# Output projection of the last row tile placed ahead of the turning of four other tiles (hybrid decoder layer, one core)

## The chip, the cores and the metric

The kernel runs on one core of one Trainium2 chip. The metric is the device time in microseconds from the first to the last instruction of one execution. TensorE is called PE below, VectorE DVE, ScalarE ACT, GpSimd POOL and SyncE SP. Each engine works off its own instructions in a fixed order, and an instruction that waits holds up all that stand behind it on that engine. SP computes nothing here: it issues most of the loads, so its order is the order of a queue of loads.

## The reference

One layer of a decoder trunk: 1024 prompt rows (tiles 0 to 7 of 128 rows) and 64 sample rows (tile 8), 1024 features, fp32.

```python
def layer(h, p_l, ...):
    xn = rmsnorm(h, norm_mix)
    mix = token_mixers(xn, ...)        # two groups of heads, then: concat([o_ret, o_rw], -1) @ w_out
    h = h + mix
    h = h + peer(rmsnorm(h, norm_ffn), peer_wq, peer_keys, peer_u, peer_v)
    gate = sigmoid(rmsnorm(h, ple_norm) @ ple_gate)
    return h + gate * (p_l @ ple_proj)

def peer(xn, wq, keys, u_tab, v_tab):                  # 8 heads, 2 x 128 keys, 16 picks
    q = (xn @ wq).reshape(rows, 8, 2, 128)
    s = einsum('phcd,hcnd->phcn', q, keys)
    sv, si = top_k(s, 16)                              # then the best 16 of the 256 pairs: e, gsm
    hval = einsum('pd,phkd->phk', xn, u_tab[e])
    return einsum('phk,phkd->pd', gelu(hval) * gsm, v_tab[e])
```

The retention heads (`o_ret`) and the RWKV-7 heads (`o_rw`) of a tile need the state that the tile before leaves, so the tiles go through the mixers one after the other.

## The kernel before

**Stages.** First the mixers, tile by tile, tile 7 last. Beside them the rows of finished tiles go through `c_rows`: the output projection (`ewo`, 1024 x 1024 weights `cw`, loaded anew for each tile), the residual add, the store of the row to the DRAM array `hd`, the norm, and the store of the normed row to `xd`. Then the query stage: `c_query` runs over 16 half heads; for each it loads 512 KB of `wq` (`wqr`), splits it into a high part on ACT (`wqh`) and a low part on POOL (`wql`), multiplies it with the turned rows of six tiles (`pq`: 256 columns for group G1, tiles 2 and 3, and 512 columns for group G2, tiles 4 to 7) and scores it against the keys (`psc`); DVE then picks the best 16 (`MAX8`, `FIND_INDEX8`, `MATCH_REPLACE8`, lines 1043 to 1047). After it come the hidden stage and the dense stage, in which G2 is computed against all 16384 experts (`ph`, `py`), and the last stage, `ple`, tile by tile in the order 0, 1, 8, 4, 5, 6, 7, 2, 3.

**Turning.** The query needs the normed rows with features on the partitions, each split in two parts. `split_T` does it for one tile: eight 128 x 128 transposes on PE (`ntr`, line 326) into two PSUM banks of tag "a", and for each bank the high part on ACT (line 303) and the low part on DVE (line 305), both named `cx`. `rows_in` loads a tile's normed row from `xd` into a buffer `cxn` (line 1010) and turns it. Tag "a" has two PSUM banks, tag "b" three.

**The gather.** Tiles 0, 1, 8 and then 2, 3 go through the experts that they picked, one expert row at a time: POOL issues an indirect load of 512 KB (`grow`, line 1144) into one of about five buffers, DVE works it in with one instruction (line 1158 in the first pass, `gacc`, line 1172, in the second). One such piece of work is called a gather step here. The steps have the lowest priority of all, and a scheduler that works at build time on the order of emission and priorities puts them between the other instructions. That order is fixed when the kernel runs. A gather's result is stored (`yd`) and added to its tile's rows at line 1413 in `ple`.

**The seam.** The change is in what lies between tile 7's mixers and the query. The last vector operation of the mixers is line 989: `tail`, the gated RWKV half of tile 7's rows. The gate's matmul goes to a bank `pgt` of tag "a" (`PGT = "a"`), which is held until `tail` has read it. `tail` stays on the chip. Around it `build()` emits:

1. `rows_in` for G1 (tiles 2 and 3), with two `cxn` buffers (`CN = 2`);
2. `rest()`, the `c_rows` of the other late tiles, of which tile 6 is the last;
3. `c_rows` of tile 7, here called the last tile's rows. It differs from the others: all eight weight slabs `cw` (512 KB each, line 589) are loaded at once into buffers that the query uses later; the tile's residual row is loaded to `ch` (line 594, one of the two buffers of tag `uraw` that the query's `wqr` also uses); the row `od` of the retention half is loaded to `cot`; both halves are transposed (`etr`, line 604); the projection is 16 matmuls of 128 x 512 (line 611); DVE adds the two halves of the result to `ch` (line 613); `ch` is stored to `hd`, squared on ACT (`csq`, line 627), the norm's factor is made on POOL (`crs`, lines 297 and 298), DVE multiplies (line 633) and `split_T` turns `ch` itself (`ntr<-ch`);
4. between its steps, one tile of `rows_in` for tiles 4, 5 and 6;
5. the query, and then what is left of the early gathers.

`tail`, the eight `cw` and tile 7's `ch` meet in one more place: seven of the eight `cw` slabs go to buffers whose former content `tail`'s stage has to be done with, so that their loads wait for `tail`.

Of the kernel before, what the change touches and what calls it, by code (L numbers as in the profile page):

```python
# [8 lines left out]
F32 = mybir.dt.float32  # L9
# [8 lines left out]
D = 1024  # L18
# [164 lines left out]
G1 = [2, 3]  # L183
DW = 4
LW = 3
CN = 2
BORDER = [1, 8, 2, 3, 4, 5, 6, 7]
A0 = [0, 1]
A1 = [2, 3]
# [2 lines left out]
PGT = "a"  # L192
# [3 lines left out]
G2 = [4, 5, 6, 7]  # L196
# [9 lines left out]
def spans(tiles):  # L206

    e = [sum(SIZE[t] for t in tiles[:i]) for i in range(len(tiles) + 1)]
    return dict(zip(tiles, e)), e[-1]
# [8 lines left out]
class K:  # L218
# [360 lines left out]
    def c_rows(self, wp, t, ring=4, da=None, x=None):  # L579

        nc, I = self.nc, self.I
        n = SIZE[t]
# [18 lines left out]
        for k in range(2):  # L601
            p = self.ps("etr", "a").rearrange("p (a b) -> p a b", a=4)
# [4 lines left out]
        if da is not None:  # L607
            p = [self.ps("ewo", "b") for _ in range(2)]
            for k in range(8):
                for c in range(2):  # L610
                    nc.tensor.matmul(p[c][:n], oT[k // 4][:, k % 4, :n], ws[k][:, cs[c]], start=k == 0, stop=k == 7)
            for c in range(2):
                nc.vector.tensor_tensor(h[:n, cs[c]], p[c][:n], h[:n, cs[c]], op=OP.add)
        else:
            for c in range(2):
                p = self.ps("ewo", "a")
                for k in range(8):
                    w = half("cw")
                    nc.sync.dma_start(w, I['w_out'][k, :, cs[c]])
                    nc.tensor.matmul(p[:n], oT[k // 4][:, k % 4, :n], w, start=k == 0, stop=k == 7)  # L620
                    if k % 4 == 3:
                        yield
                nc.vector.tensor_tensor(h[:n, cs[c]], p[:n], h[:n, cs[c]], op=OP.add)
# [7 lines left out]
        for c in range(2):  # L631
            nc.sync.dma_start(gr[c], I['rows'][o + 512 * c:o + 512 * c + 512].partition_broadcast(128))
            nc.vector.scalar_tensor_tensor(h[:n, cs[c]], h[:n, cs[c]], r[:n], gr[c][:n], op0=OP.mult, op1=OP.mult)
        if x is not None:
            self.split_T(h, n, x[0], x[1], 0)
        else:
            nc.scalar.dma_start(self.xd[t][:n], h[:n])
# [66 lines left out]
    def rw_mix(self, t):  # L704
        nc, I, O, wp = self.nc, self.I, self.O, self.cw
        smp = t == 8
        n, o = SIZE[t], t * 128
# [3 lines left out]
        hb = "bd" if smp or first else "bb"  # L711
# [9 lines left out]
        p = self.ps("pz")  # L721
# [12 lines left out]
        for k in range(2):  # L734
            p = self.ps("pcs")[:, :258].rearrange("p (a b) -> p a b", a=2)
# [10 lines left out]
        p = self.ps("pa").rearrange("p (a b) -> p a b", a=4)  # L746
# [21 lines left out]
        p = self.ps("pbon")  # L768
# [70 lines left out]
        for li, m in enumerate(LEVELS):  # L839
# [4 lines left out]
            for s in range(2):  # L844
                p = self.ps("trz", hb[s]).rearrange("p (a b) -> p a b", a=4)
# [4 lines left out]
                p = self.ps("pG", hb[s])[:, :256].rearrange("p (h q) -> p h q", h=4)  # L850
# [5 lines left out]
            for s in range(2):  # L856
                p = self.ps("pZG", hb[s])[:, :256].rearrange("p (h q) -> p h q", h=4)
# [20 lines left out]
        p = self.ps("pX", "d")  # L878
# [12 lines left out]
        if smp:  # L891
            p = self.ps("pU", "d")
# [5 lines left out]
        else:  # L898
            lo, up = slice(0, 64), slice(64, 128)
            for half in (lo, up):  # L900
                if half is up:
                    p = self.ps("pL", "d")
# [5 lines left out]
                p = self.ps("pU", "d")  # L908
# [5 lines left out]
        if not smp:  # L914
            p = self.ps("pS", "d").rearrange("p (a b) -> p a b", a=4)
# [15 lines left out]
            if t == 7:  # L931
                p = self.ps("pso", "d").rearrange("p (a b) -> p a b", a=4)
# [7 lines left out]
        else:  # L940
# [6 lines left out]
            for h in range(8):  # L947
                hs = slice(h * 64, h * 64 + 64)
                p = self.ps("pss", "b")
# [32 lines left out]
        bv = T3("bv").rearrange("p (h d) -> p h d", h=8)  # L982
        nc.vector.tensor_tensor(bv[:n], V[:n].rearrange("p (h d) -> p h d", h=8), bon[:n, 8:16, None].to_broadcast([n, 8, 64]), op=OP.mult)
        eng.tensor_tensor(xc[:n], xc[:n], bv[:n], op=OP.add)
        p = self.ps("pgt", PGT or hb[0])
        nc.tensor.matmul(p[:n], sf13[:, :n], self.g2, start=True, stop=True)
        if t == 7:
            self.tail = self.ep0.tile([128, 512], F32, name="tail", tag="Wq", bufs=QB)
# [14 lines left out]

    def rows_in(self, wp, tiles, x):

        off, _ = spans(tiles)
        for t in tiles:
            n = SIZE[t]
            xn = wp.tile([128, D], F32, name="cxn", bufs=CN)
            self.nc.sync.dma_start(xn[:n], self.xd[t][:n])  # L1010
            self.split_T(xn, n, x[0], x[1], off[t])
            yield

    def c_query(self, wp, da, parts):
# [429 lines left out]
    def build(self):  # L1444
        PS = bass.MemoryType.PSUM
        run = lambda g: [None for _ in g]
        sb = lambda name, es, **kw: self.pool(name, es=es, reuse_waits="tile", **kw)
        with self.es:
            self.setup()
            em, ee, eg, et, ew, ex, ep, e0, e1, e2 = (ExitStack() for _ in range(10))  # L1450
# [26 lines left out]
            for _ in a:  # L1477
                for _ in range(IE):
                    next(early, None)
            e2.close()  # L1480
            late = self.group_b(BORDER, early)
            em.close()
            cq = sb("cq", ew, bufs=2, side="right")
            parts = [G1, G2]
            self.layout(cq, [(f"ss{g[0]}", [128, len(g), 128], F32, SB) for g in parts] +
                        [(f"qT{g[0]}", [128, spans(g)[1]], F32, 1) for g in parts])
            cn = sb("cn", ew, side="right")
            c1 = sb("cx1", ew, side="right")
            x1 = self.rows_of(c1, G1)
            cx = sb("cx2", ex)  # L1490
            x = self.rows_of(cx, G2)
# [8 lines left out]
            def rest():  # L1500
                for t in late[:-1]:
                    yield from self.c_rows(co, t, CRING)

            run(self.rows_in(cn, G1, x1))
            run(rest())
            last = self.c_rows(co, late[-1], CRING, da, [y[:, :, n3:] for y in x])
            next(last)
            for _ in self.rows_in(cn, G2[:-1], x):
                next(last, None)
            run(last)  # L1510
            run(query)
            run(early)
# [12 lines left out]
            with ExitStack() as e:  # L1525
# [9 lines left out]
                for i, t in enumerate(G2 + [None]):  # L1535
                    tk = self.topk(tp, t) if t is not None else iter(())
                    while True:
                        a, b = next(tk, "end"), next(gate, "end")
# [41 lines left out]
```

## Time and profile before

| | us |
|---|---|
| three runs: lowest, median, highest | 3747.6, 3758.44, 3776.36 |
| the profiled execution, its own time | 3747.65 |
| its span in the trace | 3745.9 |
| PE busy | 3294.1 (88%) |
| DVE busy | 2856.0 (76%) |
| POOL busy | 2336.2 (62%) |
| ACT busy | 1217.6 (33%) |

The span is 1.75 us shorter than the execution's own time, and the execution is one of the fastest of the runs. "Idle before" in a row of a trace is the time in which the engine stood still ahead of an instruction, and the arrow names what ended it. Rows of a timeline give the start and the duration, and several equal instructions in one row have a joint duration.

### The profile page before, as it was taken

How to read it: one execution, taken by the hardware profiler on the slowest of the kernel's cores; microseconds unless marked ns; L12 is line 12 of the kernel's file. 1: busy time of each engine (PE TensorE's matmuls, PEld its weight loads, DVE VectorE, ACT ScalarE, POOL GpSimd, SP SyncE). 2: the span in 40 equal slices, each digit the busy share in tenths (PEclk: the TensorE clock that was granted, in tenths of full speed). 3: DMA queues.
4: the chain of work that ended last, by engine and by line, in shares of the span. 5: the costliest groups of instructions: out<-in, count | busy, mean ns of one | idle time of the engine just before them, and what ended most of it. 6: DMA issues, size and time to landing. Idle time of an engine off the chain costs nothing. (4 is left out here: it accounts for less than half of the span.)

```text
span 3745.9 us, 52394 instructions
## 1 busy us (share of the span) xinstructions
PE 3294.1 (88%) x17749; PEld 2742.5 (73%) x17749; DVE 2856.0 (76%) x5655; ACT 1217.6 (33%) x2260; POOL 2336.2 (62%) x2068
## 2 busy tenths in 40 slices
PE   7799995868869978884899999998999999989979
PEld 7698994644747866673787888887888877767757
DVE  4454388878797698886897998875777787888885
ACT  4232220111202111211222788793333333333322
POOL 5364176455364555554558877867888888888751
PEclk9799995667968566876999999999999999999989
DMA  7266578889778877888769888899999999999982
GB/s 254 81 216 212 187 244 289 276 286 311 258 249 313 311 268 253 285 273 320 254 216 317 298 311 320 332 340 334 337 347 342 328 354 371 374 370 368 339 279 89
DMA packets 425286, 1077.84 MB, mean 288 GB/s; under 512 B 46459, under 2 KB 144505, under 8 KB 420346
## 3 DMA queue, kind: packets, MB, share of 16 engines
q0 software_dynamic: 165888, 604.05, 45.5%
q1 hardware_dynamic: 203102, 378.60, 30.6%
q10 hardware_dynamic: 56028, 91.84, 6.6%
q8 instruction: 141, 2.31, 0.2%
q14 instruction: 127, 1.04, 0.1%
HBM read 982.51 MB, written 91.75 MB: 287 GB/s over the span
## 5 line engine op out<-in xcount | busy, mean ns | idle before, releaser
L1144 POOL DMA_INDIRECT grow<-in_pv,eid x576 | 567.4, 985 | 464.1 <-DVE gacc L1172 289.0
L1144 POOL DMA_INDIRECT grow<-in_pu,eid x576 | 558.1, 969 | 405.6 <-DVE grow L1158 228.0
L1172 DVE SCALAR_TENSOR_TENSOR gacc<-grow,ac,gacc 128x1024 f32<-128x1024 f32 x571 | 731.8, 1282 | 87.0 <-DMA grow<-in_pv,eid 80.3
L1158 DVE SCALAR_TENSOR_TENSOR grow<-grow,gacc 128x1024 f32<-128x1024 f32 x576 | 691.6, 1213 | 131.0 <-DMA grow<-in_pu,eid 124.1
L332 PE MATMUL ph<-cx,uh 128*128 128x512 f32 x1024 | 406.3, 397 | 17.5 <-DVE al L305 9.8
L1318 PE MATMUL py<-ah,vh 128*128 128x512 f32 x1024 | 403.3, 394 | 19.7 <-ACT vh L303 19.7
L333 PE MATMUL ph<-cx,uh 128*128 128x512 f32 x1024 | 404.9, 395 | 0.0
L1319 PE MATMUL py<-al,vh 128*128 128x512 f32 x1024 | 402.4, 393 | 2.6 <-DVE al L305 2.6
L307 POOL TENSOR_TENSOR vl<-vraw,vh 128x640 fp32r<-128x640 f32 (+1 forms) x224 | 326.2, 1460 | 34.9 <-ACT vh L303 17.5
L307 POOL TENSOR_TENSOR ul<-uraw,uh 128x1024 fp32r<-128x1024 f32 x128 | 307.7, 2404 | 64.5 <-issue 26.8
L1321 PE MATMUL py<-ah,vl 128*128 128x512 f32 x1024 | 275.9, 397 | 11.4 <-POOL vl L307 11.1
L335 PE MATMUL ph<-cx,ul 128*128 128x512 f32 x1024 | 263.2, 395 | 2.9 <-POOL ul L307 2.9
L303 ACT ACTIVATE vh<-vraw 128x640 fp32r<-128x640 f32 (+1 forms) x224 | 154.9, 692 | 301.8 <-DMA vraw<-in_pvd 105.6
L1318 PEld LDWEIGHTS py<-ah,vh 128*128 128x128 f32 x1024 | 193.5, 189 | 68.5 <-ACT vh L303 27.0
L332 PEld LDWEIGHTS ph<-cx,uh 128*128 128x128 f32 x1024 | 194.5, 190 | 58.0 <-DVE al L305 10.2
L1321 PEld LDWEIGHTS py<-ah,vl 128*128 128x128 f32 x1024 | 191.5, 189 | 61.7 <-POOL vl L307 20.7
L1319 PEld LDWEIGHTS py<-al,vh 128*128 128x128 f32 x1024 | 193.8, 189 | 44.4 <-DVE al L305 3.9
L1325 DVE TENSOR_TENSOR yT<-yT,py 128x512 f32<-128x512 f32 x216 | 147.7, 684 | 98.2 <-PE py L1321 86.8
L333 PEld LDWEIGHTS ph<-cx,uh 128*128 128x128 f32 x1024 | 194.4, 190 | 38.4
L335 PEld LDWEIGHTS ph<-cx,ul 128*128 128x128 f32 x1024 | 191.1, 189 | 42.0 <-POOL ul L307 4.0
L307 POOL TENSOR_TENSOR wl<-wraw,wh 128x1024 fp32r<-128x1024 f32 x45 | 114.7, 2550 | 114.2 <-ACT wh L303 96.3
L303 ACT ACTIVATE uh<-uraw 128x1024 fp32r<-128x1024 f32 x128 | 135.2, 1056 | 151.8 <-DMA uraw<-in_puT 91.4
(401 smaller groups left out, 7352.7 us busy)
## 6 DMA issues: line engine op xcount, KB each, us to landing
uraw<-in_puT SPq DMA_DIRECT2D x128, 512.0 KB
vraw<-in_pvd SPq DMA_DIRECT2D x128, 320.0 KB
cw<-in_w_out SPq DMA_DIRECT2D x128, 256.0 KB
wd<-wst ACTq DMA_DIRECT2D x28, 1024.0 KB
wt<-wd SPq DMA_DIRECT2D x64, 448.0 KB
wraw<-in_w_ret SPq DMA_DIRECT2D x48, 512.0 KB
ewq<-in_wq SPq DMA_DIRECT2D x48, 512.0 KB
vraw<-in_pvd SPq DMA_DIRECT2D x96, 256.0 KB
```

What stands on the lines that cost most here:

```text
L303: nc.scalar.activation(hi, src, AF.Copy)
L307: nc.gpsimd.tensor_tensor(lo, src, hi.bitcast(F32), op=OP.subtract)
L332: mm(out, lh(k), rh(k), start=first and k == 0, stop=False)
L333: mm(out, *((ll(k), rh(k)) if right else (lh(k), rl(k))), start=False, stop=False)
L335: mm(out, *((lh(k), rl(k)) if right else (ll(k), rh(k))), start=False, stop=last and k == nk - 1)
L1144: nc.gpsimd.indirect_dma_start(out=g, out_offset=None, in_=src, in_offset=bass.IndirectOffsetOnAxis(ap=self.eid[t][:, j:j + 1], axis=0))
L1158: nc.vector.scalar_tensor_tensor(g[:, c], g[:, c], 1.0, x[:, c], op0=OP.mult, op1=OP.mult, accum_out=hv[:, i, j:j + 1])
L1172: nc.vector.scalar_tensor_tensor(y[:, c], g[:, c], ac[:, j:j + 1], y[:, c], op0=OP.mult, op1=OP.add)
L1318: nc.tensor.matmul(p, vh[:, b, :], ah, start=b == 0, stop=False)
L1319: nc.tensor.matmul(p, vh[:, b, :], al, start=False, stop=False)
L1321: nc.tensor.matmul(p, vl[:, b, :], ah, start=False, stop=b == nb - 1)
L1325: nc.vector.tensor_tensor(yT[:, d, :], yT[:, d, :], p, op=OP.add)
```

## The change

- The two `cxn` buffers become four (`CN`), and their pool is opened right after the mixers' pool is closed, ahead of the query's pool `cq`.
- The gate's bank `pgt` of tile 7 is one of the three banks of tag "b".
- `c_rows` gets two more stops (`yield`): one behind the two adds of the last tile, one ahead of its `split_T`.
- `build()` emits `rest()` first, then two steps of the last tile's rows (its loads), the turning of tile 2, three steps of the last tile's rows (transposes, projection, adds), the turning of tiles 3, 4 and 5, one step (the norm), the turning of tile 6, and the turning of tile 7. Then the query follows, as before.

```diff
-CN = 2
+CN = 4
...
             for c in range(2):
                 nc.vector.tensor_tensor(h[:n, cs[c]], p[c][:n], h[:n, cs[c]], op=OP.add)
+            yield
...
         if x is not None:
+            yield
             self.split_T(h, n, x[0], x[1], 0)
...
-        p = self.ps("pgt", PGT or hb[0])
+        p = self.ps("pgt", "b" if t == 7 else PGT)
...
-        off, _ = spans(tiles)
+        off = {**spans(G1)[0], **spans(G2)[0]}
...
-            self.split_T(xn, n, x[0], x[1], off[t])
+            self.split_T(xn, n, *x[t], off[t])
...
+            cn = sb("cn", ew, side="right")
+            self.layout(cn, [("cxn", [128, D], F32, CN)])
             cq = sb("cq", ew, bufs=2, side="right")
...
-            cn = sb("cn", ew, side="right")
...
-            run(self.rows_in(cn, G1, x1))
+            ahead = self.rows_in(cn, G1 + G2[:-1], dict([(t, x1) for t in G1] + [(t, x) for t in G2]))
             run(rest())
             last = self.c_rows(co, late[-1], CRING, da, [y[:, :, n3:] for y in x])
+            for _ in range(2):
+                next(last)
+            next(ahead)
+            for _ in range(3):
+                next(last)
+            for _ in range(3):
+                next(ahead)
             next(last)
-            for _ in self.rows_in(cn, G2[:-1], x):
-                next(last, None)
+            run(ahead)
             run(last)
```

Since the scheduler decides the order, it is shown for three places. The rows give the line, the operation, the tiles and how many follow each other. In the changed kernel lines behind 612 have numbers that are one or two higher (633 becomes 634, 1010 becomes 1012, 1172 becomes 1174).

**PE at the seam**, before. `ntr<-csta,cxn` are transposes of tiles 2 to 6, `etr` those of tile 7's two halves, `ewo` its projection; the long row of `pq` work ahead of these is left out:

```order
L335 MATMUL pq<-cx_13013,wql 128x256 x8
L604 MATMUL etr<-csta,tail 128x128 x4
L611 MATMUL ewo<-cw,coT 128x512 x8
L326 MATMUL ntr<-csta,ch 128x128 x8
L332 MATMUL pq<-cx_13018,wqh 128x512
```

and now:

```order
L604 MATMUL etr<-csta,cot 128x128 x4
L604 MATMUL etr<-csta,tail 128x128 x4
L611 MATMUL ewo<-cw,coT 128x512 x2
L326 MATMUL ntr<-csta,cxn 128x128 x8
L611 MATMUL ewo<-cw,coT 128x512 x6
L326 MATMUL ntr<-csta,cxn 128x128 x8
L611 MATMUL ewo<-cw,coT 128x512 x6
L326 MATMUL ntr<-csta,cxn 128x128 x8
L611 MATMUL ewo<-cw,coT 128x512 x2
L326 MATMUL ntr<-csta,cxn 128x128 x8
L332 MATMUL pq<-cx_13014,wqh 128x256
```

Before, the 40 transposes of tiles 2 to 6, the first eight matmuls of the projection and the first G1 part of the query stand ahead of the transposes of `tail`. Now the 32 transposes of tiles 3 to 6 stand between and behind the matmuls of the projection, and the transposes of tile 2 stand ahead of the rows shown; the query's first 24 matmuls come behind the projection.

**SP around tile 7's weights**, before. `od_99` is tile 7's retention half, `xd_85` to `xd_89` the normed rows of tiles 2 to 6:

```order
L599 DMA cot<-od_99 128x512
L1010 DMA cxn<-xd_85 128x1024
L1010 DMA cxn<-xd_86 128x1024
L589 DMA cw<-in_w_out 128x1024 x8
L594 DMA ch<-in_x 128x1024
L1021 DMA wqr<-in_wq 128x1024
L1010 DMA cxn<-xd_87 128x1024
L1010 DMA cxn<-xd_88 128x1024
L1010 DMA cxn<-xd_89 128x1024
L1021 DMA wqr<-in_wq 128x1024 x3
L632 DMA cgr<-in_rows 128x512 x2
```

and now:

```order
L599 DMA cot<-od_99 128x512
L1012 DMA cxn<-xd_89 128x1024
L589 DMA cw<-in_w_out 128x1024 x8
L594 DMA ch<-in_x 128x1024
L1021 DMA keysT<-in_keysT 128x128
L1023 DMA wqr<-in_wq 128x1024
L1021 DMA keysT<-in_keysT 128x128
L633 DMA cgr<-in_rows 128x512 x2
L1023 DMA wqr<-in_wq 128x1024 x5
```

The loads of tiles 2 to 5 have gone up into the loads of tiles 5 and 6's projections. Tile 6's load stands ahead of the eight `cw` now, and the residual row `ch` still behind them.

**DVE around `tail` and the adds**, before (`cx` is a low part of the turning, `gacc` a gather step):

```order
L989 TENSOR_TENSOR tail<-hnx,pgt 128x512
L1172 SCALAR_TENSOR_TENSOR gacc<-grow,ac,gacc 128x1024 x4
L305 TENSOR_TENSOR cx_13014<-ntr,cx_13013 128x4x128 x4
L1172 SCALAR_TENSOR_TENSOR gacc<-grow,ac,gacc 128x1024 x4
L305 TENSOR_TENSOR cx_13019<-ntr,cx_13018 128x4x128 x2
...
L1172 SCALAR_TENSOR_TENSOR gacc<-grow,ac,gacc 128x1024 x5
L613 TENSOR_TENSOR ch<-ewo,ch 128x512 x2
L1172 SCALAR_TENSOR_TENSOR gacc<-grow,ac,gacc 128x1024 x4
L633 SCALAR_TENSOR_TENSOR ch<-ch,crs,cgr 128x512 x2
```

and now:

```order
L991 TENSOR_TENSOR tail<-hnx,pgt 128x512
L1174 SCALAR_TENSOR_TENSOR gacc<-grow,ac,gacc 128x1024
L305 TENSOR_TENSOR cx_13015<-ntr,cx_13014 128x4x128 x2
L1174 SCALAR_TENSOR_TENSOR gacc<-grow,ac,gacc 128x1024 x3
L305 TENSOR_TENSOR cx_13015<-ntr,cx_13014 128x4x128 x2
...
L613 TENSOR_TENSOR ch<-ewo,ch 128x512 x2
L1174 SCALAR_TENSOR_TENSOR gacc<-grow,ac,gacc 128x1024
L305 TENSOR_TENSOR cx_13020<-ntr,cx_13019 128x4x128 x2
L1174 SCALAR_TENSOR_TENSOR gacc<-grow,ac,gacc 128x1024 x3
L634 SCALAR_TENSOR_TENSOR ch<-ch,crs,cgr 128x512 x2
```

Between `tail` and the adds stand 6 gather steps where there were 22; between the adds and the multiplications 4 as before, and two low parts more. From `tail` to the query's first `MAX` it is 14 steps instead of 30. Between the copy of the RWKV state (`wkvo`) and `tail` stand 11 steps, before 10. At the end of the program, behind the last `yT` addition of the dense stage, 46 gather steps stand where there were 31, between the same instructions of `ple`; the last one stands ahead of tile 7's first `psg` multiplication.

## The prediction

> **What bounds the kernel now.** I read the page's totals first, then the waits of PE, then PE's timeline where they are large.
>
> ```profile
> span 3745.9 us, 52394 instructions
> PE 3294.1 (88%) x17749; PEld 2742.5 (73%) x17749; DVE 2856.0 (76%) x5655; ACT 1217.6 (33%) x2260; POOL 2336.2 (62%) x2068
> ```
>
> PE is the fullest engine, so a change helps where PE stands still. One such place is the seam between tile 7's mixers and the query. PE's waits from 1700 to 1810 us:
>
> ```profile
> PE ntr L326 <- DMA cxn<-xd: 18.2, 2, 15.9
> PE ntr L326 <- DVE tail L989: 16.5, 1, 16.5
> PE ntr L326 <- issue: 13.1, 1, 13.1
> PE ntr L326 <- DVE cx L305: 8.9, 2, 8.4
> ```
>
> The columns are the sum, the times and the longest. All four stand before transposes. In PE's timeline they are here:
>
> ```profile
> 1713.08 1.12 PE L326 MATMUL ntr<-csta,cxn 128*128 128x128 f32 x4 [2.33 <-DMA cxn<-xd]
> 1730.65 1.11 PE L326 MATMUL ntr<-csta,cxn 128*128 128x128 f32 x4 [16.45 <-DVE tail L989]
> 1740.14 1.97 PE L326 MATMUL ntr<-csta,cxn 128*128 128x128 f32 x8 [8.38 <-DVE cx L305]
> 1758.01 1.94 PE L326 MATMUL ntr<-csta,cxn 128*128 128x128 f32 x8 [15.90 <-DMA cxn<-xd]
> 1764.95 9.63 PE L611 MATMUL ewo<-cw,coT 128*128 128x512 f32 x16 [0.69 <-ACT coT L605]
> 1780.49 7.13 PE L611 MATMUL ewo<-cw,coT 128*128 128x512 f32 x16 [1.72 <-ACT coT L605]
> 1800.70 2.10 PE L326 MATMUL ntr<-csta,ch 128*128 128x128 f32 x8 [13.07 <-issue]
> 1802.47 1.01 PE L332 MATMUL pq<-cx,wqh 128*128 128x512 f32 x2
> ```
>
> From 1802.47 on the query runs with all six tiles. Ahead of that, tile 2's second half waits for the bank that `tail` holds, tile 4 for its rows, and the projection stands behind both. The engine that ends the last wait is DVE:
>
> ```profile
> 1728.72 1.28 DVE L1172 SCALAR_TENSOR_TENSOR gacc<-grow,ac,gacc 128x1024 f32<-128x1024 f32 x1
> 1729.92 0.68 DVE L989 TENSOR_TENSOR tail<-hnx,pgt 128x512 f32<-128x512 f32 x1
> 1788.63 1.28 DVE L613 TENSOR_TENSOR ch<-ewo,ch 128x512 f32<-128x512 f32 x2
> 1789.82 3.93 DVE L1172 SCALAR_TENSOR_TENSOR gacc<-grow,ac,gacc 128x1024 f32<-128x1024 f32 x3
> 1798.65 1.29 DVE L1172 SCALAR_TENSOR_TENSOR gacc<-grow,ac,gacc 128x1024 f32<-128x1024 f32 x1 [4.90 <-DMA grow<-in_pv,eid]
> 1799.85 0.74 DVE L633 SCALAR_TENSOR_TENSOR ch<-ch,crs,cgr 128x512 f32<-128x512 f32 x1
> ```
>
> `tail` ends at 1729.92 + 0.68 = 1730.6, and 58 us later the adds run. Between the adds and the multiplication stand four gather steps, the last of them 4.9 us late for its row. So the seam is a chain: `tail`, weights, projection, adds, norm, turning. And the windows show the transfers in it and the clock granted to PE (the columns: window, its length, busy us of PE, PEld, DVE, ACT, POOL with counts, clock, DMA share, GB/s):
>
> ```profile
> 1745.00:1758.00 13.00, 0.00 (x0) 0.02 (x1) 3.57 (x3) 0.00 (x0) 3.71 (x4) 0.50 1.03 409
> 1766.00:1769.00 3.00, 3.00 (x5) 1.31 (x4) 2.65 (x3) 0.23 (x1) 1.90 (x3) 0.50 0.74 221
> 1772.00:1775.00 3.00, 3.00 (x13) 1.52 (x12) 1.99 (x2) 0.00 (x0) 2.60 (x2) 1.00 0.80 255
> 1840.00:1900.00 60.00, 60.00 (x375) 53.89 (x374) 60.00 (x300) 19.35 (x33) 32.31 (x25) 1.00 0.69 225
> 2000.00:2080.00 80.00, 70.52 (x299) 56.07 (x298) 56.28 (x105) 23.77 (x34) 70.30 (x53) 0.98 0.92 320
> 2560.00:3575.00 1015.00, 971.49 (x4179) 785.61 (x4177) 792.11 (x1175) 346.96 (x546) 833.33 (x685) 0.99 0.98 349
> 3650.00:3700.00 50.00, 48.81 (x239) 40.46 (x238) 37.78 (x52) 18.77 (x34) 8.57 (x17) 1.00 0.40 132
> ```
>
> While PE is empty (1745 to 1758) the DMA engines are full: the seam is bound by loads there. Behind 1802 PE is busy nearly all the time, so an earlier start of the query is worth its full length if nothing later gives it back.
>
> **The change part by part.** I count from `tail`'s end, T, and first ask what moves T. One gather step more stands ahead of `tail`, 1.28 us: T = 1731.9. The transposes of tile 2 now stand between PE's last mixer matmuls, where 8 of them cost 2 us by the row of 1740.14; `tail` waits for DVE in that stretch and not for PE, so I put that at nothing, and at 2 us if it doesn't hide.
>
> *The bank.* With `pgt` in tag "b", the 16.45 us wait of tile 2's second half is gone. By itself it frees little, because the loads behind `tail` still come; I give it no time of its own.
>
> *The loads.* SP's timeline around `tail`:
>
> ```profile
> 1714.99 19.27 SPq L589 DMA_DIRECT2D cw<-in_w_out  x8
> 1734.30 0.49 SPq L594 DMA_DIRECT2D ch<-in_x  x1
> 1737.09 0.33 SPq L1021 DMA_DIRECT2D wqr<-in_wq  x1
> 1738.89 21.40 SPq L1010 DMA_DIRECT2D cxn<-xd  x3
> SPq L589 <- DVE tail L989: 15.2, 1, 15.2
> SPq L1010 <- DMA hd<-ch: 10.4, 1, 10.4
> ```
>
> The last two rows are SP's waits. One `cw` goes out at 1715, then SP waits 15.2 us for `tail`. Behind it come seven `cw`, `ch`, one `wqr` and the first `cxn` of the three (tile 4's rows), whose landing lets PE go on at 1758.01. Ten loads of 512 KB in 1758.01 − 1730.6 = 27.4 us are 2.74 us each. Now four row loads go out before `tail` and the fifth ahead of the weights; behind `tail` stand seven `cw` and `ch`. The projection needs the `cw` only, the adds also `ch`: 8 × 2.74 = 21.9, so `ch` is there at T + 21.9. In between PE has 8 `etr`, 16 `ewo` and 24 transposes of tiles 3 to 5. At the fast rate these are 7.13 + 24 × 0.25 + 2 = 15 us; they fit, and the last pair of `ewo` can end before `ch` lands. The adds end at T + 21.9 + 1.3 = T + 23.2.
>
> *The adds to the multiplication.* Before: 1799.85 − (1788.63 + 1.28) = 9.94 us. The chain itself is shorter: POOL's last part of the norm's factor was done by 1793.2.
>
> ```profile
> 1792.65 0.57 POOL L298 TENSOR_TENSOR crs<-crs,halves 128x1 f32<-128x1 f32 x1
> L1172 DVE SCALAR_TENSOR_TENSOR gacc<-grow,ac,gacc x30: 1276/1289/1290, 1731.4 to 1806.7; 128x1024 f32<-128x1024 f32 x30
> ```
>
> So the gather steps set it. The second row groups the 30 steps from `tail` to the first pick: 1.28 us of work each, one in 75.3 / 29 = 2.6 us. Now only 6 stand in the 22 us ahead of the adds, one in 3.7 us; their rows should lie ready, and the four run without a wait. Four steps and two low parts of 0.64 us are 6.4 us, the lower bound. The upper is the measured 9.94 plus the two low parts, 11.2. I take 7.5, near the lower one, since what made the difference was the late row. The multiplication starts at T + 30.7.
>
> *To the query.* From the multiplication to the first full `pq` it was 1802.47 − 1799.85 = 2.62 us, and stays. On ACT a split of the second `wq` load now stands ahead of the turning's high parts: 1 us if its load is there; 0 and 6 are the bounds (the 6: two loads of 2.74). I take 1. The query goes at T + 34.3 = 1766.2 instead of 1802.47. **The seam gets 36.3 us shorter.**
>
> *What is given back.* The gather steps that ran in the hole don't vanish. 16 steps fewer stand between `tail` and the first pick, and 15 more behind the dense stage, where the table of the order shows 46 for 31. They need DVE 15 × 1.28 = 19.2 us. The rows of the end:
>
> ```profile
> L1172 DVE SCALAR_TENSOR_TENSOR gacc<-grow,ac,gacc x32: 1272/1278/1290, 3575.1 to 3664.4; 128x1024 f32<-128x1024 f32 x32
> 3664.36 1.27 DVE L1172 SCALAR_TENSOR_TENSOR gacc<-grow,ac,gacc 128x1024 f32<-128x1024 f32 x1
> 3704.68 1.23 DVE L1413 TENSOR_TENSOR ph<-ph,py 128x1024 f32<-128x1024 f32 x1 [1.26 <-DMA ph<-hd]
> ```
>
> The last step ends at 3665.6, and its result is not needed before 3704.68: 39 us of slack. Between 3650 and 3700 DVE stands idle 50 − 37.78 = 12.2 us while PE is busy 48.81 of 50. So 12 of the 19.2 us go into idle time, and the rest, 7, may come between PE and its next operand; I take 6, with 0 (all hidden) and 19 (none) as the bounds. In the middle four steps or so are carried through the query, where DVE is as full as PE (60.00 of 60 in 1840 to 1900); 4 × 1.28 = 5.1. From 2000 on DVE is busy 56.28 of 80 and gives 23.7 us of room, so I take 1, with 0 and 5 as the bounds. In the dense stage (2560 to 3575) DVE is idle 223 of 1015 us and hides the rest.
>
> The sum: 36.3 − 6 − 1 = 29.3 us less, from the profiled execution's own 3747.65: 3718.3. That execution is the fastest of those shown but for 0.05 us, and the runs' median lies 10.8 us higher; a median that lies as high would be 3729. I write 3722, between the two, nearer to the profiled one.
>
> **A rule that speaks against it.** In the seam PE ran at a clock of 0.50 and came to 1.00 only in 1772 to 1775, some 9 us after its work had closed up; the `ewo` began at 0.50. The change spreads the projection between loads. The Trainium skill (TensorE: Matmul & The Clock Gate, "HAM oscillation — how this bites in real kernels") says that where each block's matmuls are shorter than the wait for the next slab of weights, PE falls back to the half clock in every block and starts each one cold. By that rule the clock stays at 0.50 from `tail` to the query here. By the row of 1764.95, whose full-speed counterpart takes 7.13, it would add little if the pair per load stays under 2.74 us; the first rival prices it.
>
> **The rivals.**
>
> 1. *PE at half clock becomes the bound of the seam.* At 0.50 the transposes take 0.25 us each (1.97 for 8). The longest `ewo`, at the start, took 1.22:
>
> ```profile
> L611 PE MATMUL ewo<-cw,coT x16: 592/592/1222, 1764.9 to 1774.0; 128*128 128x512 f32 x16
> ```
>
>  If all sixteen take that, one behind the other, PE needs 16 × 1.22 + 24 × 0.25 + 2 = 27.5 us, begun 4 us behind `tail`: T + 31.5, 9.6 later than the loads. For it: the clock of 0.50. Against it: five `ewo` fit in 3 us at 0.50 (1766 to 1769), 0.6 each. Time: 3718 + 10 = 3728. Chance 0.08.
> 2. *The last gather sets the end.* If a step costs the 2.9 us that lie between steps today (89.3 / 31), 15 take 43 us; the slack of 39 less some 9 for store and load is 30. 13 come back instead of 6: 3725. For it: no other work fills POOL there (8.57 of 50), yet steps are 2.9 apart. Against it: they are apart because the order puts them so. Chance 0.12.
> 3. *SP's head.* Tile 6's rows stand ahead of all eight `cw` and wait for their own store, issued on ACT when the row is finished. Before, a `cxn` load waited 10.4 us for such a store. Should it hold back the weights past `tail`, up to 10 come on top: 3728. Against it: that store went out 12 us ahead of `tail`:
>
> ```profile
> 1718.18 0.34 ACTq L637 DMA_DIRECT2D xd<-ch  x1
> ```
>
>  Chance 0.10.
> 4. *The other side: the gather stream has no slack and every deferred step comes back at full price.* If the loads for the gather bound everything behind the seam (DMA share 0.98 in the dense stage), the 19 steps by which the stream trails at the first pick (16, and 3 from ahead of `tail`) cost their spacing of 2.6 us: 49.4, against 36.3. Time: 3747.65 + 13 = 3761, slower. It decides once a deferred step costs over 36.3 / 19 = 1.9 us of the end. Against it: PE, not DMA, is closed up there (971 of 1015), and the end has room on every engine. Chance 0.06.
> 5. *More is won.* The bounds on the good side: 6.4 for the four steps, no wait for the split, nothing given back: 36.3 + 1.1 + 1 = 38.4, 3709. For it: 39 us of slack at the end. Chance 0.18.
>
> **How the numbers follow.** The forecast has 0.46. The range runs from rival 5 with a few us for runs, 3705, to 3752, which takes in rivals 1 to 3, both upper bounds of what is given back (19 and 5: 3735) and the 10.8 us of the median; most of rival 4 is outside. A measurement of this kernel tells about 1%, 37.5 us, from no change; the runs shown span 0.8%. Over 1% faster needs most of rival 5 and the good edge of the forecast: 0.18 + 0.06 = 0.24. Over 1% slower is beyond even rival 4's price: 0.03. Within 1%: 0.73.
>
> **What would show it.** Right: no wait on `tail` before transposes of tile 2; the `cw` landing 2.7 us apart and the adds 22 us behind `tail`; about 7 us from adds to multiplication; the first 512-wide `pq` near 1766; the last gather step behind 3665 counted from the old end, with DVE near full in the last stage. Wrong by rival 1: `ewo` back to back, `ch` long landed. Rival 2: `ph<-ph,py` of tile 3 waiting for `py<-yd`. Rival 3: the first `cw` issued behind `tail`. Rival 4: PE waits in the dense stage that grow with the gather.

## The result and the profile after

The changed kernel took 3726.47 us (median of 4 runs, 3709.06 to 3733.49), the kernel before in the same comparison 3767.4: a ratio of 0.9885 (95% interval 0.9851 to 0.9918). Timed again on another occasion it was 0.9889 (0.9862 to 0.9915; 3724.53 of 6 runs against 3764.03 of 18). So it is faster by 1.1%, 42 us by the second ratio (the medians lie 41 and 39.5 us apart), with 32 us as the near end of its interval. The two profiled executions, 3747.65 and 3727.77, are only 19.9 us apart; why is in the part on what was right and wrong.

PE at the seam in the changed kernel, the same stretch as shown of before (the rows of the mixers, of tile 6's turning and of the query's first part are left out):

```profile
1714.03 0.66 PE L326 MATMUL ntr<-csta,cxn 128*128 128x128 f32 x4
1743.06 1.11 PE L604 MATMUL etr<-csta,cot 128*128 128x128 f32 x4 [22.56 <-DVE cx L305]
1743.96 1.06 PE L604 MATMUL etr<-csta,tail 128*128 128x128 f32 x4
1744.86 3.78 PE L611 MATMUL ewo<-cw,coT 128*128 128x512 f32 x4
1748.43 1.27 PE L326 MATMUL ntr<-csta,cxn 128*128 128x128 f32 x8
1749.54 5.32 PE L611 MATMUL ewo<-cw,coT 128*128 128x512 f32 x12
1754.69 1.04 PE L326 MATMUL ntr<-csta,cxn 128*128 128x128 f32 x8
1755.57 5.32 PE L611 MATMUL ewo<-cw,coT 128*128 128x512 f32 x12
1760.72 1.04 PE L326 MATMUL ntr<-csta,cxn 128*128 128x128 f32 x8
1761.59 1.88 PE L611 MATMUL ewo<-cw,coT 128*128 128x512 f32 x4
1773.26 1.94 PE L326 MATMUL ntr<-csta,ch 128*128 128x128 f32 x8 [2.65 <-issue]
1775.04 1.01 PE L332 MATMUL pq<-cx,wqh 128*128 128x512 f32 x2
```

and DVE there (rows left out in the same way):

```profile
1740.53 0.68 DVE L991 TENSOR_TENSOR tail<-hnx,pgt 128x512 f32<-128x512 f32 x1
1741.13 1.28 DVE L1174 SCALAR_TENSOR_TENSOR gacc<-grow,ac,gacc 128x1024 f32<-128x1024 f32 x1
1742.32 1.28 DVE L305 TENSOR_TENSOR cx<-ntr,cx 128x512 fp32r<-128x512 f32 x2
1763.19 1.28 DVE L613 TENSOR_TENSOR ch<-ewo,ch 128x512 f32<-128x512 f32 x2
1764.38 1.28 DVE L1174 SCALAR_TENSOR_TENSOR gacc<-grow,ac,gacc 128x1024 f32<-128x1024 f32 x1
1767.37 1.29 DVE L305 TENSOR_TENSOR cx<-ntr,cx 128x512 fp32r<-128x512 f32 x2 [1.71 <-ACT cx L303]
1768.58 3.93 DVE L1174 SCALAR_TENSOR_TENSOR gacc<-grow,ac,gacc 128x1024 f32<-128x1024 f32 x3
1772.41 1.41 DVE L634 SCALAR_TENSOR_TENSOR ch<-ch,crs,cgr 128x512 f32<-128x512 f32 x2
```

`tail` ends at 1741.2, the adds begin 22.0 us behind it, the multiplication 7.9 us behind the adds' end (1772.41 − 1764.47), and the first 512-wide `pq` 33.8 us behind `tail`. Before, this last stretch was 71.9. One wait is left in the first part: PE stands 22.56 us ahead of tile 7's transposes, no longer for `tail` itself but for the low parts of tile 2 (1742.32), which DVE's order puts just behind `tail`.

### The profile page after: what moved, and what is told of

It is laid out like the page before. It is cut to its first block, busy times and chain, and to the rows that moved or that the text cites. A ratio compares the mean times of both kernels' runs of the same rounds, so it can differ in the third digit from the quotient of the medians.

```text
span 3725.8 us, 52387 instructions
## 1 busy us (share of the span) xinstructions
PE 3296.6 (88%) x17749; PEld 2739.2 (74%) x17749; DVE 2842.5 (76%) x5655; ACT 1217.8 (33%) x2260; POOL 2337.0 (63%) x2068
## 5 line engine op out<-in xcount | busy, mean ns | idle before, releaser
L1323 PE MATMUL py<-ah,vl 128*128 128x512 f32 x1024 | 273.9, 397 | 10.5 <-POOL vl L307 10.3
```

The costliest lines, as they stand in the source:

```text
L1323: nc.tensor.matmul(p, vl[:, b, :], ah, start=False, stop=b == nb - 1)
```

## The experiments

My theory (A) was that the order makes the gain: what hangs on `tail` goes first, and what doesn't stands behind. The rivals were that the bank does it (B), whose wait was the longest but one in the list, or the buffers (C), with which the rows come early. So the three parts of the change were tried apart and in two of the three pairs; order and bank with two `cxn` buffers was not run. The early opening of the `cxn` pool is in every kernel below but the bank alone, so it isn't parted from the rest. A stretch that starts at `tail`'s end doesn't see what a run loses or gains ahead of it. Two such stretches, to the first 512-wide `pq` and to the last `pq`, stand in the table beside the timed ratio (to before, with the 95% interval, 7 to 12 us to each side). The stretches come from one trace each where no second is given.

| kernel | `tail` to first 512-wide `pq`, us | `tail` to last `pq`, us | ratio |
|---|---|---|---|
| before, two traces | 71.9, 73.3 | 225.5, 226.8 | |
| bank alone (e1) | 72.3 | 226.4 | 0.9978 (0.9959 to 0.9997) |
| buffers alone (e2) | 54.7 | 209.3 | 0.9951 (0.9924 to 0.9978) |
| bank and buffers (e10) | 48.0 | 201.5 | 0.9934 (0.9911 to 0.9958) |
| order alone (e9) | 38.5 | 191.1 | 0.9946 (0.9922 to 0.9970) |
| order and buffers (e4) | 36.6 | 191.5 | 0.9919 (0.9896 to 0.9942) |
| the change, two traces | 33.8, 33.8 | 192.2, 190.0 | 0.9889 (0.9862 to 0.9915) |
| five slabs early (e8) | 31.2 | 185.3 | 0.9896 (0.9863 to 0.9929) |
| turning first (e11) | 44.1 | 198.3 | 0.9966 (0.9944 to 0.9988) |

**The change and the kernel before once more** (no edit).

> The changed kernel once more, for a narrower interval and a second trace. From tail's end to the first 512-wide pq it took 33.8 us in its first profile, against 71.9 before. If that stretch is set by the program's order, it comes back within 2 us (32 to 36); the ratio to before then lies between 0.985 and 0.993 (the seam's 38 us less some 7 given back, 0.8%, and what single runs vary by). If the first profile's ratio of 0.9885 came from a lucky set of runs, it falls to 0.995 or above.

> The kernel before once more, for a second trace. From tail's end to the first 512-wide pq it took 71.9 us in the first; if the order sets it, it comes back within 3 us. Its time then was 3747.65, and the runs' median is 16 us higher; in the first trace the clock was granted in full at 800 to 820 us, where the changed kernel, with the same instructions in the same order there, had 0.50 and fell 9 us behind. If that is chance, a second trace shows tail's end some 5 to 15 us later than 1730.6 and the last stage again at 168 to 173 us; if the 16 us arise behind the seam, tail's end is at 1730 again.

The stretch came back at 33.8 us, and before at 73.3. The ratio stayed. `tail`'s end in before's second trace was at 1740.3, 10 us later than in the first, and the execution took 3771.08. So the first trace of before was a quick one ahead of the seam, and its 3747.65 isn't the right base for a difference.

**The bank alone.** In before:

```diff
-        p = self.ps("pgt", PGT or hb[0])
+        p = self.ps("pgt", "b" if t == 7 else PGT)
```

> Before, with only the bank of tile 7's gate moved to tag b. Theory A (order): the seam is set by the loads behind tail and by what PE does after them; tile 2 is turned earlier, but tile 4's rows still come tenth behind tail, so that tail's end to the first 512-wide pq stays at 66 to 72 us and the time within 0.3% of before. Rival B (bank): the 16.5 us wait on tail was part of the path, and the stretch falls to about 55 us, the time by 0.4%.

72.3 us, a little outside the 66 to 72 expected of theory A and far from theory B's 55. In time it was 0.2%, with an interval that just misses no change. PE's waits from 1700 to 1815 in this kernel:

```profile
PE ntr L326 <- DVE cx L305: 25.4, 2, 24.9
PE ntr L326 <- DMA cxn<-xd: 16.0, 1, 16.0
PE ntr L326 <- issue: 12.5, 1, 12.5
```

The wait of 16.5 us for `tail` is gone from the list, and one of 24.9 us for the low part stands there instead. PE got on earlier by one half tile and then met the next operation that DVE does behind `tail`. The wait for tile 4's rows is what it was (16.0, before 15.9).

**The buffers alone.** In before:

```diff
-CN = 2
+CN = 4
...
+            cn = sb("cn", ew, side="right")
+            self.layout(cn, [("cxn", [128, D], F32, CN)])
             cq = sb("cq", ew, bufs=2, side="right")
...
-            cn = sb("cn", ew, side="right")
```

> Before, with only the four cxn buffers and their pool opened early; the order of emission is the old one, the gate's bank too. Rows of four tiles load ahead of tail, so PE needn't wait for the tenth load. Theory A (order): turning, then half the projection, then a part of the query still come ahead of the transposes of tail, so the adds come some 36 us behind tail, and the stretch to the first 512-wide pq is about 50 us (45 to 56): a good half of the gain, 0.5%. Rival C (buffers): the early rows are the whole gain, the stretch is 34 to 40 us and the time as that of the changed kernel.

54.7 us, in the range of theory A, and 0.49% in time, a little under half of the gain. PE no longer waits for the tenth load, but works off the old order:

```profile
1742.85 1.11 PE L326 MATMUL ntr<-csta,cxn 128*128 128x128 f32 x4 [15.68 <-DVE tail L989]
1752.79 1.97 PE L326 MATMUL ntr<-csta,cxn 128*128 128x128 f32 x8 [2.21 <-DVE cx L305]
1757.11 9.54 PE L611 MATMUL ewo<-cw,coT 128*128 128x512 f32 x16 [0.69 <-ACT coT L605]
1772.96 7.03 PE L611 MATMUL ewo<-cw,coT 128*128 128x512 f32 x16
```

The projection begins at 1757.11, 14 us behind `tail`, since the turning of tile 2's second half and of three more tiles stands ahead of it, and its second half behind a part of the query.

**Bank and buffers.** The two diffs together, with the old order.

> Before, with the bank and the four early buffers, and the old order of emission. Alone the bank gave nothing (72.3 us) and the buffers 17 (54.7). Theory A (order): with both, the turning of tiles 3 to 6 still stands ahead of the projection on PE, and goes at the pace of two banks and DVE's low parts; the stretch is 44 to 52 us, the bank worth 3 to 10 now that the rows are there in time. Rival (bank and buffers are all of it): 33 to 37 us.

48.0 us. The bank, worth nothing in the stretch alone, is worth 6.7 us where the rows are there in time. It doesn't take the order's place.

**The order alone.** The changed kernel with

```diff
-CN = 4
+CN = 2
...
-        p = self.ps("pgt", "b" if t == 7 else PGT)
+        p = self.ps("pgt", PGT or hb[0])
```

> The changed kernel with two cxn buffers and the gate's bank in tag a: only the order of emission and the early pool are left of the change. The projection stands ahead of tiles 4 to 6, but their rows now load behind tail again, behind the weights and the residual row. Theory A (order): the adds come 22 to 26 us behind tail as in the changed kernel; the first 512-wide pq then waits for the eleventh load behind tail (11 times 2.74, 30 us) and tile 6's turning: 38 to 46 us from tail's end, the time 0.6 to 0.9% below before. Rival C (buffers): without the four buffers the stretch is above 55 us.

38.5 us: of the 39 us that the seam gives, the order by itself brings 34. The 38.5 flatters it a little, since the first 512-wide `pq` came here when only four of the eight transposes of tile 7's row were done; the other four began 2.5 us behind it. But at the last `pq` it was level with the change, 191.1 us. The parts overlap, so the 34 is no share of a sum: bank and buffers bring 25 without the order, and the order then adds 14. In time the order alone was 0.54% (0.30 to 0.78), less than the 0.6 to 0.9 I expected and not to be told from the buffers alone (0.49%). In its trace the change's gain is missing behind the last `pq`, in the hidden and dense stages (see the next section). Here PE had fewer transposes between the pairs of the projection and met the weights' pace:

```profile
1768.64 1.98 PE L611 MATMUL ewo<-cw,coT 128*128 128x512 f32 x4 [0.15 <-DMA cw<-in_w_out]
1771.21 1.98 PE L611 MATMUL ewo<-cw,coT 128*128 128x512 f32 x4 [0.59 <-DMA cw<-in_w_out]
1773.74 1.98 PE L611 MATMUL ewo<-cw,coT 128*128 128x512 f32 x4 [0.55 <-DMA cw<-in_w_out]
1776.30 1.98 PE L611 MATMUL ewo<-cw,coT 128*128 128x512 f32 x4 [0.58 <-DMA cw<-in_w_out]
```

One slab comes each 2.55 us ((1776.30 − 1768.64) / 3), and PE needs 1.98 for its pair.

**Order and buffers, without the bank.** The changed kernel with the second of those two edits.

> The changed kernel with the gate's bank put back to tag a. Theory A (order): the bank by itself is worth little, since PE now waits for a free bank of tag a in any case until DVE has worked in tile 2's low parts just behind tail; the stretch is 34 to 40 us and the time within 0.3% of the changed kernel. Rival B (bank): the stretch is 45 us or more and most of the gain is lost.

36.6 us; the bank is worth 2.8 us of the seam at the end. The time was 0.30% above the changed kernel's, which the two intervals don't tell from nothing.

**Five slabs early.** Seven of the eight slabs wait for `tail`. By my reading of the buffers' layout, which no trace shows, only two of them lie where `tail`'s input lay, and the others are queued behind the first of these on SP. This kernel deals the buffers out anew:

```diff
-            for k in range(8):
-                ws.append(da.tile([128, D], F32, name="cw", **(dict(tag="spare", bufs=1) if k == 7 else dict(tag=("uh", "ul")[k % 2], bufs=(DW, LW)[k % 2]))))
+            for k in range(5):
+                ws.append(da.tile([128, D], F32, name="cw", **(dict(tag="spare", bufs=1) if k == 4 else dict(tag="uh", bufs=DW))))
                 nc.sync.dma_start(ws[k], I['w_out'][k])
...
         nc.sync.dma_start(h[:n], I['x'][t * 128:t * 128 + n])
+        if da is not None:
+            for k in range(5, 8):
+                ws.append(da.tile([128, D], F32, name="cw", tag="ul", bufs=LW))
+                nc.sync.dma_start(ws[k], I['w_out'][k])
...
-            self.layout(da, [("uh", [128, 8, 128], F32R, DW), ("ul", [128, 8, 128], F32R, LW), ("uraw", [128, 8, 128], F32, UB), ("spare", [128, 8, 128], F32, 1)])
+            self.layout(da, [("uraw", [128, 8, 128], F32, UB), ("spare", [128, 8, 128], F32, 1), ("ul", [128, 8, 128], F32R, LW), ("uh", [128, 8, 128], F32R, DW)])
```

> The changed kernel with the weights of tile 7's projection dealt out anew over the same buffers: five of the eight slabs and the residual row go to buffers that tail's inputs don't lie in, and are issued ahead of the three that do. So only three loads wait for tail instead of eight; PE's order stays nearly as it was. Theory L (the loads set the 22 us from tail's end to the adds): three loads are 8.2 us, and the adds come 12 to 16 us behind tail. Theory P (PE sets it: 32 records of ewo at 0.45 us and 32 transposes at 0.13, with no gap, begun 1.9 us behind tail): the adds stay at 20 to 23 us, and the time stays within 0.2% of the changed kernel.

SP in this kernel:

```profile
1713.65 3.28 SPq L589 DMA_DIRECT2D cw<-in_w_out  x5
1716.97 0.66 SPq L594 DMA_DIRECT2D ch<-in_x  x1
1726.88 1.28 SPq L598 DMA_DIRECT2D cw<-in_w_out  x3
```

DVE and PE:

```profile
1726.13 0.68 DVE L995 TENSOR_TENSOR tail<-hnx,pgt 128x512 f32<-128x512 f32 x1
1748.26 0.68 DVE L617 TENSOR_TENSOR ch<-ewo,ch 128x512 f32<-128x512 f32 x1
```

```profile
1729.48 1.12 PE L608 MATMUL etr<-csta,cot 128*128 128x128 f32 x4 [23.48 <-DVE cx L305]
```

The loads went out 10 to 13 us ahead of `tail`, only three behind it, and the adds still came 21.4 us behind it. PE ran from 1729.48 without a wait, as in the changed kernel. Theory P holds here: PE alone fills those 22 us. The kernel's time is that of the changed kernel; it doesn't beat it.

**Turning first.** The changed kernel with tiles 2 to 5 emitted ahead of the projection:

```diff
-            next(ahead)
-            for _ in range(3):
-                next(last)
-            for _ in range(3):
-                next(ahead)
-            next(last)
+            for _ in range(4):
+                next(ahead)
+            for _ in range(4):
+                next(last)
```

> The changed kernel with tiles 2 to 5 all emitted ahead of tile 7's transposes and projection, since PE stands idle 22.6 us ahead of tail while their rows are there. On DVE the low parts still stand behind tail, so that the two banks of tag a hold up the 24 transposes until then. Theory A: they then stand in the path: tile 7's transposes begin 10 to 12 us behind tail instead of 1.9, the adds come at 26 to 30 us instead of 22, the stretch is 37 to 42 us instead of 33.8, and the time 0 to 0.2% above the changed kernel. Rival: the idle time is used and the stretch falls to 30 us.

Its PE rows:

```profile
1764.29 1.97 PE L326 MATMUL ntr<-csta,cxn 128*128 128x128 f32 x8 [21.78 <-DVE cx L305]
1770.40 1.97 PE L326 MATMUL ntr<-csta,cxn 128*128 128x128 f32 x8 [0.67 <-DVE cx L305]
1772.93 1.11 PE L604 MATMUL etr<-csta,cot 128*128 128x128 f32 x4 [0.56 <-DVE cx L305]
1774.73 8.19 PE L611 MATMUL ewo<-cw,coT 128*128 128x512 f32 x16
```

`tail` ended at 1762.4, the transposes of tile 7 began 10.5 us later, the adds came at 27.0: as theory A had it. The idle time ahead of `tail` can't be used for turning while DVE's part of it stands behind `tail`. The rest was worse than expected: 13.0 us from the adds to the multiplication, where DVE stood 7.0 us for a late gather row, 44.1 in all against 37 to 42 expected, and a time 0.77% above the changed kernel against 0 to 0.2. That is 29 us, some 13 to each side by the two intervals, and the stretch explains 10 of them. What made the rest is open.

**The gather's last steps.** To see whether the later gather lengthens the last stage, the last 16 of 128 rows in the second pass of tile 3's gather were left out, in before and in the changed kernel:

```diff
         y = home()
-        for j in range(n):
+        m = n - 16 if t == G1[-1] else n
+        for j in range(m):
             g = fetch(I['pv'], j)
...
-            if j < n - 1:
+            if j < m - 1:
                 yield j
```

> Before, with the last 16 of the 128 rows of the second pass of tile 3's gather left out: that part of the expert sum is missing. The seam is untouched. Theory A (7 us given back in the last stage because 15 gather steps more than before stand there): before, the last stage isn't set by the gather, so leaving steps out changes little: the last stage 166 to 170 us instead of 168 to 173, the time within 0.2%.

> The changed kernel with the same 16 steps left out, so that 30 gather steps stand behind the dense stage instead of 46, about as many as before. Theory A: the 7 us come back: the last stage takes 168 to 171 us instead of 176 to 177, and the time is 6 to 9 us less than that of the changed kernel. Rival: the longer last stage comes from something else (clock, its loads): it stays at 175 us or more.

The last stage (last `yT` addition to the end) took 169.0 us in before so cut, against 169.6 and 172.9 uncut, and 172.4 in the changed kernel so cut, against 177.4 and 176.4: between theory A's 168 to 171 and the rival's 175. The times: a ratio of 0.9990 (0.9967 to 1.0013) for the first, 3718.07 us and 0.9883 (0.9842 to 0.9924) for the second. That median is 6.5 to 8.4 us under the changed kernel's, which were taken on other occasions; by the ratios to before it is 0.06%, 2 us, and either is inside the interval. So the direction is theory A's and the size some 4.5 us, from one trace, where before's two traces are 3.3 us apart. But the count isn't all: e2 with 38 steps there took 168.2, e8 with 43 took 166.3. Each kernel has its own order in this stage, and that decides as well; the experiments don't part the two.

## Why the prediction was right, and where not

**The forecast** was 29 us less, 3722; the measured 3726 lies in the range, and the mechanism is the one forecast but for a term that was mis-sized (below). That the two times are 4 us apart is luck in part: the base, 3747.65, was 16 to 20 us under before's medians, and the gain was 10 to 13 us larger than my sum; the two errors go against each other. The interval's near end, 32 us, says too that the gain is larger. Over 1% faster, as it came, had a chance of 0.24, and within 1% had 0.73. The condition that I gave for it, most of rival 5, isn't what happened: something was given back, and ten us came from stages that I had at nothing. In stages, with two traces of each kernel (before / after, us):

| | before | after | difference of the means |
|---|---|---|---|
| start to `tail`'s end | 1730.6, 1740.3 | 1741.2, 1743.1 | +6.7 |
| to the first 512-wide `pq` | 71.9, 73.3 | 33.8, 33.8 | −38.8 |
| to the last `pq` | 153.6, 153.4 | 158.4, 156.2 | +3.8 |
| to the first `py` | 631.3, 630.8 | 623.1, 626.5 | −6.3 |
| to the last `yT` addition | 988.9, 998.5 | 991.9, 987.3 | −4.1 |
| to the end | 169.6, 172.9 | 177.4, 176.4 | +5.6 |

The bounds of the stages in the changed kernel, second column of times, are rows like these:

```profile
L335 PE MATMUL pq<-cx,wql x256: 277/384/478, 1769.4 to 1933.4; 128*128 128x256 f32 x64, 128*128 128x512 f32 x64
L1320 PE MATMUL py<-ah,vh x1024: 387/389/795, 2556.5 to 3546.4; 128*128 128x512 f32 x171
L1327 DVE TENSOR_TENSOR yT<-yT,py x216: 673/686/690, 2603.5 to 3548.4; 128x512 f32<-128x512 f32 x108
```

**T.** I put `tail` 1.3 us later for one more gather step. From the copy of the RWKV state to `tail`'s end it was 25.3 and 24.3 us before, 26.1 and 26.6 after: right. The 10 us beside it in the first pair come from far ahead, most of them from a stretch in which the clock differed (last part).

**The 22 us to the adds: the number right, its reason not.** The step that failed reads "At the fast rate these are 7.13 + 24 × 0.25 + 2 = 15 us; they fit". The row of 7.13 us has 16 records, and I took it for the whole projection; its other half is the row of 9.63 above it, with 16 more. Sixteen fp32 matmuls leave 32 records. So PE needs 2 × 7.13 = 14.3 us for them at the fast rate, and with the transposes, the first 6 us at half the clock, ran from 1743.06 to some 1763.4 without a gap: 20 us, begun 1.9 us behind `tail`. The sum's 15 us left 7 us of room; there was none. By chance eight loads take as long. From `tail` to the landing of the ninth load, which ACT waited for,

```profile
1765.80 1.06 ACT L303 ACTIVATE wqh<-wqr 128x1024 fp32r<-128x1024 f32 x1 [3.36 <-DMA wqr<-in_wq]
```

it was 24.6 us, 2.73 each, so that `ch`, the eighth, was there at 1763.1 by estimate, just as PE ended. With five slabs early it was PE alone. In the change's second trace the loads came last: PE stood for a slab, and the adds for `ch`, 22.8 us behind `tail`:

```profile
1761.11 1.99 PE L611 MATMUL ewo<-cw,coT 128*128 128x512 f32 x4 [0.58 <-DMA cw<-in_w_out]
1765.87 1.29 DVE L613 TENSOR_TENSOR ch<-ewo,ch 128x512 f32<-128x512 f32 x2 [0.39 <-DMA ch<-in_x]
```

In e9, too, where PE waited for slabs 2.55 us apart, the landing of `ch` ended DVE's wait ahead of the adds, at 24.0 us. So the two bounds lie within a microsecond or so of each other, and either can be the last.

**Adds to the multiplication.** 7.5 forecast; 7.9 and 7.5. The gather rows did lie ready, as argued: three steps ran in 3.93 us with no wait for a row. What lies above the lower bound of 6.4 is another wait, 1.71 us of DVE for ACT's high part of the turning (1767.37). **To the query** 2.6 forecast and 2.6 and 2.2 measured; the 1 us for the second split wasn't there, since it lay beside the norm. The seam as a whole: 34.3 forecast from T, 33.8 measured.

**What is given back.** In the query 1 was forecast, with 5 as the bound, and 3.8 measured: in the changed kernel's first trace PE has a wait of 4.2 us there, where before it had 0.7,

```profile
PE psc L1036 <- ACT qT L1033: 4.2, 1, 4.2
```

in the last stage 6, and 5.6 measured. The last step is at 3680.9 where the last `yT` addition is at 3548.4, 132.5 us behind it, before 88. The slack that I counted (39 us) was used up almost to the end: the last tile's `ph` waited for its gather's result,

```profile
3690.49 1.23 DVE L1415 TENSOR_TENSOR ph<-ph,py 128x1024 f32<-128x1024 f32 x1 [1.59 <-DMA py<-yd]
```

which is the sign named for rival 2, 1.6 us of it. With `tail` some 1.5 us later the sum of what I priced is −38.8 + 1.5 + 3.8 + 5.6 = −27.9; forecast were −29.3. The other ten, between the last `pq` and the last `yT` addition, I had at nothing. The two kernels with the short gather differ from these only by 16 steps at the gather's end, and so give a third trace of each. The hidden and the dense stage together took 1620.2, 1629.3 and 1624.7 us before, and 1615.0, 1613.8 and 1614.7 in the changed kernel. So the ten seem to belong to the changed kernel and not to chance. What makes them is open: the order alone (1627.9), order and buffers (1628.2) and five slabs early (1633.7), one trace each, don't have them.

**The rivals.** *Half clock*: PE's clock in the windows of the changed kernel,

```profile
1743.00:1746.00 3.00, 2.94 (x10) 2.19 (x11) 2.96 (x3) 1.19 (x2) 1.56 (x2) 0.50 0.99 369
1746.00:1749.00 3.00, 3.00 (x8) 1.34 (x7) 1.41 (x2) 0.00 (x0) 1.27 (x3) 0.52 1.03 421
1749.00:1764.00 15.00, 15.00 (x58) 8.16 (x57) 6.99 (x10) 3.26 (x6) 2.50 (x3) 1.00 1.00 390
```

was 0.50 for the first 6 us and then 1.00, and PE stood without a wait. So rival 1's sign, `ewo` back to back, did come, though not `ch` long landed. PE did end with the loads or behind them, but mostly at the full clock, and because of records that I hadn't counted (rival 1 prices sixteen too, where there are 32). The rule of the Trainium skill (TensorE: Matmul & The Clock Gate, "HAM oscillation — how this bites in real kernels") speaks of blocks shorter than the wait for the next slab, a wait long enough to cross the window in which the clock gate finds PE idle; the prediction left this second condition out. No run here had such blocks: in e9 the four records of a slab took 1.98 us and the waits ahead of them 0.15 to 0.59 us. The clock granted there, from 1768 to 1780 us, was 1.00. So waits of that length did not bring the clock down here, and the rule itself is not tested. *The gather at the end*: present, and small (1.6 us of wait). *SP's head*: tile 6's rows did hold SP for 15.4 us, but the first `cw` went out at 1729.15, ahead of `tail`; no cost. *The other side*: 16 steps left out gave 4.5 us in the last stage, 0.3 us each and not over 1.9, and the dense stage didn't grow. *More is won*: the seam gave 38.8 less 1.5 for `tail`, 1 us short of the 38.4 of the good bounds, but something was given back.

## What to carry to other kernels

When a value comes late, put first what depends on it alone, and what doesn't behind; here the order of emission alone shortened the seam by 34 of 39 us, the buffers alone by 18 and the bank alone by nothing. Parts that overlap don't add up, and a gain in one stretch isn't yet one in the whole time: the order alone came to 0.54% of it and the buffers alone to 0.49%. A wait that is taken away alone shows what stands next in line: look for that before pricing it. And count records against the program before multiplying: a row's count may be half of an operation, or the double of its instructions.

## What the runs showed of the hardware that I had not expected

The same instructions in the same order ran 10 us apart ahead of the change, and most of that goes with the clock that PE was granted. Before's first trace and the changed kernel's, 800 to 820 us:

```profile
800.00:810.00 10.00, 9.88 (x63) 8.15 (x63) 6.99 (x13) 1.33 (x3) 3.99 (x6) 0.80 0.84 284
810.00:820.00 10.00, 5.06 (x12) 1.72 (x10) 9.41 (x12) 0.00 (x0) 5.87 (x6) 1.00 0.89 292
```

```profile
800.00:810.00 10.00, 10.00 (x62) 9.16 (x58) 5.43 (x7) 1.95 (x4) 2.81 (x3) 0.50 0.79 273
810.00:820.00 10.00, 10.00 (x35) 6.18 (x35) 5.25 (x11) 0.63 (x1) 2.80 (x3) 0.50 0.54 180
```

In the first, PE had half of the second ten us free; in the other it was busy for all twenty at 0.50. The load that SP issues next (`qv`, line 451) went out at 815.32 in the one and at 824.12 in the other; the one ahead of this stretch (`cot`, line 599) at 794.04 and 795.59. So 7.2 us arise in between. Why the clock was granted so differently, no trace here shows. `tail`'s end lay between 1726.8 and 1762.4 us in the thirteen traces of eleven kernels. The runs of one kernel differ by 1% and more, which is what makes a change of 40 us hard to see in one pair and plain in a stretch that starts behind it.
